# A hybrid DeltaNet, gating and Fourier step: chunk preparation a chunk ahead, a woven block inverse, and products one step behind

## The chip, the core and the metric

The kernel runs on one core of a Trainium2 chip. A core has a matrix engine (TensorE, PE in the profile; PEld is its weight load), three engines for elementwise work (VectorE or DVE, ScalarE or ACT, GpSimd or POOL) and SyncE (SP), which here only starts DMA transfers. Each engine runs its own list of instructions in order, and they wait for each other by semaphores. POOL and ACT can start transfers too. The metric is the device time of one execution in microseconds (us), lower is better.

## The reference, cut to what matters

One layer is computed for 2048 sample tokens and 128 prompt tokens, 1024 channels wide. A modulated RMSNorm gives `xn`; one input projection feeds three branches, each with its own SiLU gate; the branches are projected to 1024 channels, merged with sigmoid gates, and one output projection follows.

```python
proj = jnp.einsum('btd,de->bte', xn, w_in)
qkv, beta, dec, z_a, u_b, v_b, z_b, x_c, z_c, gates = jnp.split(proj, points, axis=-1)
# A: gated DeltaNet, forward and backward, with a triangular solve per chunk
m = eye + bc[..., :, None] * jnp.einsum('bnhik,bnhjk->bnhij', kc, kc) * dec_strict
sol = lax.linalg.triangular_solve(m, rhs, left_side=True, lower=True, unit_diagonal=True)
...
o_a = rmsnorm(o, o_norm_g) * silu(z_a)
# B: spatial gating in chunks of 128 tokens, 4 groups of 128 channels
vs = jnp.einsum('gpq,bnqgc->bnpgc', w_s, rmsnorm(v)) + b_s
o_b = u * vs * silu(z_b)
# C: Fourier mixing over a 32 x 64 grid and the 128 channels of each of 4 groups
o_c = fftn(x_c, axes=(rows, cols, channels)).real * silu(z_c)
merged = sum_n sigmoid(gates_n) * (br_n @ w_branch_n);  out = merged @ w_out
```

The outputs are the normed tokens of both groups and the prompt's final DeltaNet states.

## The kernel before, in words

**Number format.** Large products run in float16 with a split of each operand into a high and a low half (three matmuls for one product). A weight panel is loaded as float32 (`wst`, two buffers), then converted by `load_w` (L180): ACT squares it into `wlo` with a sum (L187), `scales` (L166) sends that sum through a small matmul with `ones16` (`wscb`) and shifts exponents on DVE (L173 to L177), ACT writes the high half `whi` (L189) and DVE the low half `wlo` (L190). Five converted panels are kept.

**Order of the stages.** After the modulation come the norm and transposes of the tokens with the gate of branch A, to about 150 us; the q, k, v projection with its convolution, to 438; branch B's spatial part (`for t in range(NCH)`, L893, one chunk of 128 tokens per step), to 568; branch B's gates (L913, four groups of channels by five tiles of tokens, `gate_unit`, L860), to 798; branch C (L936, four groups), to 1160; then `merge` (L1016) for branches B, C and A, to 1560, 1903 and 2157; then the output projection.

**Branch A beside them.** The DeltaNet work is a generator, `delta` (L842), advanced by `pace.tick(us)` calls inside the other stages: one step for every 1.6 us of work that the caller names. It first runs `prep` (L562) for all 17 chunks in five groups, four of four chunks and the prompt chunk last, and after each group `base_inverse` (L620); then `scan_dir` (L760) over the chunks forward and backward, where `level` (L660) builds a chunk's full 128 x 128 inverse from the 32 x 32 ones by two levels of products.

`prep` loads q, k and v of the chunk (`qr`, `kq`, L569), transposes them on TensorE, normalises q and k (square on ACT, sum on DVE, a power on POOL, L576 to L583), stores `kv` (L585), transposes k into `T` (L590), loads the decays `dc` (L594), and makes for both directions the matrices `n32` (L602) and their float16 halves `n16`, the diagonal blocks `nd` for the inverse (L604, L610) and `qk` (L616). Loads and stores all go to SP's queue but for `kT`.

`base_inverse` gathers the diagonal blocks of a group with eight loads (L633), inverts them by 31 pairs of products on DVE (L641, L642), makes a transposed copy (L645) and float16 halves of both (L649, L650), and stores the halves (`ei`, eight transfers, L655) and the float32 values (`es`, eight, L657). `level` loads them back as `ec` (L666) and `e3` (L668).

**What sets the order.** The program is recorded in the order of the Python code; a planner with an estimate of each instruction's duration then fixes the order on each engine and queue, and adds the semaphores. `tc.high_priority()` moves an instruction ahead; evictions of the product banks stand in it. There are three product banks (`ps_mm`), three for branch A and two others (`ps_x`). A pool that closes gives its memory to the next one, which then waits for the last users.

Of the kernel before, what the change touches and what calls it, by code (L numbers as in the profile page):

```python
# [110 lines left out]
def hybrid_flow_kernel(ctx: ExitStack, tc: tile.TileContext, x_prompt, x_sample, state_delta, c, c_ctx, ln_g, w_ada,  # L111
# [68 lines left out]
    def load_w(src, nkt, cols=P, hi=None, lo=None, tag="w", bufs=5):  # L180
        w = _W()
        st = sb(wp, [P, nkt, cols], "wst" if cols == P else tag + "st", bufs=2 if cols == P else 1)
        SY.dma_start(st, src.rearrange("(k p) c -> p k c", p=P))
        w.hi = sb(wp, [P, nkt, cols], tag + "hi", F16, bufs=bufs) if hi is None else hi
        w.lo = sb(wp, [P, nkt, cols], tag + "lo", F16, bufs=bufs) if lo is None else lo
# [38 lines left out]
    wdone, wnext = [], [0]  # L224

    def fetch(upto):
        while len(wdone) < min(upto, len(wlist)):
            src, nkt, tag, bufs = wlist[len(wdone)]
            wdone.append(load_w(src, nkt, tag=tag, bufs=bufs))
# [11 lines left out]
    class Pace:  # L241
# [6 lines left out]
        def tick(self, us):  # L248
            self.acc += us
# [153 lines left out]
    def decays():  # L403
# [69 lines left out]
        def rows_of(t):  # L473
            if t % 5 == 0:
                row = sb(dq, [P, 2, WB], "dc")
            elif t % 5 in (1, 2):
                row = sb(dq, [P, 1024], ("E", "Et")[t % 5 - 1]).rearrange("p (d x) -> p d x", d=2)
# [34 lines left out]
    for ct in range(12):  # L512
        w = getw(1, 2)
        for half in range(1):
# [20 lines left out]
            G.dma_start(qkvD[ct], y)  # L535
    pace.drain()
# [10 lines left out]
    GROUPS = [list(range(0, 4)), list(range(4, 8)), list(range(8, 12)), list(range(12, 16)), [16]]  # L547
    ndD = [dram(f"nd{g}", [2, P, len(ts), H, 32]) for g, ts in enumerate(GROUPS)]
    eD = [dram(f"ei{g}", [2, P, len(ts), H, P], F16) for g, ts in enumerate(GROUPS)]
    e32D = [dram(f"es{g}", [2, P, len(ts), H, 32]) for g, ts in enumerate(GROUPS)]  # L550
# [11 lines left out]
    def prep(g, ci, t):  # L562
        tok = sb(dq, [P, 2, WB], "tok")
        qr = sb(dq, [P, H, P], "qr")
        ss = sb(dq, [P, 2, H], "ss2", bufs=2)
        for part in range(3):
            ps = bank(ps_d, [P, WB])
            kq = qr if part == 0 else sb(dq, [P, H, P], "kq", bufs=2)
            SY.dma_start(kq, qkvD[part * 4:part * 4 + 4, :, chunk_off(t):chunk_off(t) + P].rearrange("h p t -> p h t"))  # L569
            for h in range(H):  # L570
                PE.transpose(ps[:, hs(h)], kq[:, h, :], ident)
            if part == 2:
                A.copy(tok[:, 1, :], ps)
                continue
            sq = sb(dq, [P, WB], "sq")
            A.activation(sq, ps, AF.Square)  # L576
            V.tensor_reduce(ss[:, part, :], h3(sq), AX.X, ALU.add)
            G.tensor_scalar(ss[:, part, :], ss[:, part, :], EPS, None, ALU.add)
            G.tensor_tensor(ss[:, part, :], ss[:, part, :], mhalf.to_broadcast([P, H]), ALU.pow)
            if part == 0:  # L580
# [310 lines left out]
    for i in range(4):  # L891
        V.tensor_copy(vinv[:, i:i + 1], vw[i].inv)
# [289 lines left out]
```

## Time and profile before

| | us |
|---|---|
| Time, median of 3 runs (range) | 2362.06 (2357.59 to 2364.58) |
| Profiled execution | 2355.22 |
| its span, first to last instruction | 2353.4 |
| TensorE busy | 2253.2 (96%) |
| VectorE busy | 1275.4 (54%) |
| ScalarE busy | 759.8 (32%) |
| GpSimd busy | 842.9 (36%) |
| Mean granted clock of TensorE | 0.985 |
| Moved by DMA | 350.39 MB, 149 GB/s on average |

"Span" runs from the first to the last instruction of the profiled execution. Groups of instructions are named by line, engine and operation, and `out<-in` are the program's names of tiles. "SPq" is SP's queue of transfers: the time in such a row is that of issuing the transfer, not that of moving its bytes. A wait is put down to the instruction that came last. The granted clock is the share of full speed that TensorE was given in that time: 1.00 or 0.50 here.

### The profile page before, as it was taken

How to read it: one execution, taken by the hardware profiler on the slowest of the kernel's cores; microseconds unless marked ns; L12 is line 12 of the kernel's file. 1: busy time of each engine (PE TensorE's matmuls, PEld its weight loads, DVE VectorE, ACT ScalarE, POOL GpSimd, SP SyncE). 2: the span in 40 equal slices, each digit the busy share in tenths (PEclk: the TensorE clock that was granted, in tenths of full speed). 3: DMA queues.
4: the chain of work that ended last, by engine and by line, in shares of the span. 5: the costliest groups of instructions: out<-in, count | busy, mean ns of one | idle time of the engine just before them, and what ended most of it. 6: DMA issues, size and time to landing. Idle time of an engine off the chain costs nothing. (4 is left out here: it accounts for less than half of the span.)

```text
span 2353.4 us, 43324 instructions
## 1 busy us (share of the span) xinstructions
PE 2253.2 (96%) x17092; PEld 1374.5 (58%) x17092; DVE 1275.4 (54%) x3015; ACT 759.8 (32%) x1426; POOL 842.9 (36%) x1056
## 2 busy tenths in 40 slices
PE   7999999999989987899989999999999999999998
PEld 3554444897545767779656656656665444444443
DVE  5638743568474867465665556665654242232444
ACT  3545533323323332232322222242322142221332
POOL 2422621344334430454422334455543112122543
PEclk9999999999999999999999999999999999999999
DMA  8316622575867662344444444565553353332542
GB/s 277 134 51 218 229 78 80 162 214 148 242 165 225 175 162 55 92 139 139 145 156 134 137 148 144 171 217 164 176 162 102 103 169 115 106 108 76 190 148 98
DMA packets 353237, 350.39 MB, mean 149 GB/s; under 512 B 70929, under 2 KB 273674, under 8 KB 351498
## 3 DMA queue, kind: packets, MB, share of 16 engines
q1 hardware_dynamic: 338986, 294.13, 41.6%
q0 software_dynamic: 9152, 40.13, 4.4%
q10 hardware_dynamic: 4896, 13.37, 1.6%
q8 instruction: 134, 2.20, 0.4%
q14 instruction: 69, 0.57, 0.1%
HBM read 222.16 MB, written 125.39 MB: 148 GB/s over the span
## 5 line engine op out<-in xcount | busy, mean ns | idle before, releaser
L160 PE MATMUL b<-xh,whi 128*128 128x512 f16 (+1 forms) x2080 | 704.1, 348 | 7.9 <-DVE sg L869 5.2
L160 PE MATMUL b<-xl,whi 128*128 128x512 f16 (+1 forms) x2080 | 705.2, 348 | 0.5 <-POOL xl L379 0.4
L160 PE MATMUL b<-xh,wlo 128*128 128x512 f16 (+1 forms) x2080 | 704.4, 348 | 0.2 <-DVE wlo L190 0.2
L160 PEld LDWEIGHTS <-whi 128*128 128x128 f16 x4160 | 389.0, 98 | 385.9 <-issue 17.4
L160 PEld LDWEIGHTS <-wlo 128*128 128x128 f16 x2080 | 204.1, 98 | 192.8 <-issue 5.3
L160 PE MATMUL b<-big,bhi 128*128 128x512 f16 (+1 forms) x960 | 252.6, 348 | 4.4 <-ACT big L1012 4.1
L1044 POOL TENSOR_TENSOR mrow<-mrow,sg 128x512 f32<-128x512 f32 (+1 forms) x80 | 88.0, 1104 | 316.0 <-DVE sg L1043 230.7
L160 PE MATMUL b<-whi,xh 128*128 128x128 f16 x1088 | 191.7, 222 | 1.5 <-DVE sg L869 1.5
L160 PE MATMUL b<-whi,xl 128*128 128x128 f16 x1088 | 191.8, 222 | 0.0
L160 PE MATMUL b<-wlo,xh 128*128 128x128 f16 x1088 | 191.8, 222 | 0.0
L160 PEld LDWEIGHTS <-xh 128*128 128x128 f16 x2312 | 179.6, 99 | 8.4 <-issue 7.4
L1034 ACT ACTIVATE sg<-b,winv 128x512 f32<-128x512 f32 (+1 forms) x120 | 74.6, 622 | 310.1 <-PE b L160 306.6
L160 PE MATMUL b<-big,blo 128*128 128x512 f16 (+1 forms) x480 | 163.5, 348 | 0.0
L1043 DVE SCALAR_TENSOR_TENSOR sg<-b,binv,sg 128x512 f32<-128x512 f32 (+1 forms) x80 | 53.4, 669 | 184.5 <-PE b L160 182.2
L777 POOL TENSOR_SCALAR skn<-skn,ed 128x128 f32<-128x128 f32 x136 | 81.1, 611 | 175.8 <-DMA skn<-kv 171.3
L534 POOL TENSOR_TENSOR cy<-cy,raw 128x545 f32<-128x545 f32 (+1 forms) x48 | 74.9, 1585 | 180.3 <-ACT raw L533 180.3
L160 PEld LDWEIGHTS <-bhi 128*128 128x128 f16 x960 | 89.3, 98 | 84.0 <-ACT big L1012 2.3
L160 PEld LDWEIGHTS <-xl 128*128 128x128 f16 x1224 | 115.2, 99 | 0.4
L677 POOL TENSOR_TENSOR R<-ec,cst 128x512 f16<-128x512 f16 x68 | 72.6, 1088 | 104.3 <-PE b L160 65.5
L160 PE MATMUL b<-wohi,mh 128*128 128x512 f16 x272 | 104.1, 383 | 2.1 <-ACT mh L1089 2.1
L160 PE MATMUL b<-wohi,ml 128*128 128x512 f16 x272 | 104.0, 383 | 1.6 <-DVE ml L1090 1.6
L160 PE MATMUL b<-wolo,mh 128*128 128x512 f16 x272 | 104.1, 383 | 0.0
(377 smaller groups left out, 3718.4 us busy)
## 6 DMA issues: line engine op xcount, KB each, us to landing
wst<-in_w_in_dram SPq DMA_DIRECT2D x60, 512.0 KB
qkv<-cy POOLq DMA_DIRECT2D x12, 1089.0 KB, 4.4
mrow<-br SPq DMA_DIRECT2D x24, 512.0 KB
mrow<-mrg SPq DMA_DIRECT2D x19, 512.0 KB
mrow<-mrg SPq DMA_DIRECT2D x16, 576.0 KB
mrg<-mrow POOLq DMA_DIRECT2D x16, 576.0 KB, 3.2
dc<-dec SPq DMA_DIRECT2D x17, 512.0 KB
kq<-qkv SPq DMA_DIRECT2D x34, 256.0 KB
```

Source lines behind the costliest of these rows:

```text
L160: PE.matmul(out, l, r, start=start, stop=stop)
L534: G.tensor_tensor(y[:, c0:c1], y[:, c0:c1], raw[:, 1 + c0:1 + c1], ALU.mult)
L677: G.tensor_tensor(dst[:, l].rearrange("p h a b c -> p h (a b) c"), wide(ec[:, :, which ^ d, l, :]), bm, ALU.mult)
L777: G.tensor_scalar(kn_[:, hs(h)], kn_[:, hs(h)], ed[:, d, t, h:h + 1], None, ALU.mult)
L1034: A.activation(sg, ps, AF.Sigmoid, scale=gw.inv)
L1043: V.scalar_tensor_tensor(sg, ps, binv[:, 1:2], sg, ALU.mult, ALU.mult)
L1044: G.tensor_tensor(mr, mr, sg, ALU.add)
```

## The change

Matmuls and their operands are the same, apart from how the 32 x 32 inverses reach `level`.

- **Chunk preparation.** While a chunk is prepared, the loads of the next one are issued (`held`; `rows`, `decay_rows`; `kq` three buffers, `qr` and `dc` two). k is now turned first, then v, then q. `kv` and `nd` are stored from POOL; the stores of `n16` and `qk` are held back by one (`late`). The prompt chunk comes first, as group 0.
- **Block inverse.** `base_inverse` of a group is woven between the steps of the next group's chunks. It keeps float32: the two copies are interleaved in `XB` and stored by eight transfers in four steps; `es` goes. `level` loads one float32 tile and makes the halves itself.
- **Weights.** `read_w` issues a panel's load, `convert` does the rest; `Pace.tick` issues reads up to two panels ahead, at the third tick after a conversion. The projection panels of the branches (`b`) are converted only once their own pool is open, with the first merge.
- **Branch B.** `w_spatial` is loaded at the end of the q, k, v stage. The product with `wsT` stands one chunk behind the projection, its store two more. The gate stage loads a whole row of 2176 tokens per group (`vrow`), a group ahead, instead of five pieces.
- **Branch C.** Its constants are loaded ahead of branch B. The first product of a step stands behind the next step's projection; the second and third are staggered in the same way.

```diff
+    def convert(st, nkt, cols=P, hi=None, lo=None, tag="w", bufs=5):
+        w = _W()
+        wpool = bwp[0] if tag == "b" else wp
...
+    def read_next():
+        if len(wread) < min(len(wdone) + 2, len(wlist)):
+            src, nkt, tag, bufs = wlist[len(wread)]
+            wread.append(read_w(src, nkt))
     def fetch(upto):
         while len(wdone) < min(upto, len(wlist)):
             src, nkt, tag, bufs = wlist[len(wdone)]
-            wdone.append(load_w(src, nkt, tag=tag, bufs=bufs))
+            if tag == "b" and not bwp:
+                return
+            if len(wread) == len(wdone):
+                read_next()
+            wdone.append(convert(wread[len(wdone)], nkt, tag=tag, bufs=bufs))
+            wlate[0] = 3
...
         def tick(self, us):
+            wlate[0] -= 1
+            if wlate[0] <= 0:
+                read_next()
...
+    wsn = sb(ep, [P, WB], "st", bufs=3).rearrange("p (g q) -> p g q", g=4)
+    SY.dma_start(wsn, w_spatial[0].rearrange("g p q -> p g q"))
...
-    GROUPS = [list(range(0, 4)), list(range(4, 8)), list(range(8, 12)), list(range(12, 16)), [16]]
+    GROUPS = [[16], list(range(0, 4)), list(range(4, 8)), list(range(8, 12)), list(range(12, 16))]
...
+    def late(dst, src):
+        if owed:
+            SY.dma_start(*owed.pop())
+        if dst is not None:
+            owed.append((dst, src))
+    def prep(g, ci, t, nxt, held):
...
+        more(1, lambda: rows(1, nxt))
+        more(0, lambda: rows(0, nxt))
+        ps = turned(1)
+        norm(ps, 1)
...
+        A.copy(tok[:, 1, :], turned(2))
+        more("dc", lambda: decay_rows(nxt))
+        norm(turned(0), 0)
...
-        SY.dma_start(kvD[t], tok)
+        G.dma_start(kvD[t], tok)
...
-            SY.dma_start(nD[d][t], n16)
+            late(nD[d][t], n16)
             yield 1
-        SY.dma_start(ndD[g][:, :, ci].rearrange("d p h i -> p d h i"), nd)
+        G.dma_start(ndD[g][:, :, ci].rearrange("d p h i -> p d h i"), nd)
...
     def base_inverse(g):
...
+        for _ in range(5):
+            yield 0
...
-        e16 = sb(dq, [P, 32, 2, 2, 32], "XB", F16)
-        for w_, src in enumerate((E, tmp)):
-            A.activation(e16[:, :, w_, 0, :], b3(src), AF.Copy, scale=FS)
-            V.scalar_tensor_tensor(e16[:, :, w_, 1, :], b3(src), FS, e16[:, :, w_, 0, :], ALU.mult, ALU.subtract)
+        both = XB.rearrange("p (j w c) -> p j w c", j=32, w=2)
+        V.tensor_copy(both[:, :, 1, :], E.rearrange("p (i j) -> p j i", j=32))
+        A.copy(both[:, :, 0, :], b3(E))
         yield 1
         for d in range(2):
             for B in range(4):
                 p0_ = d * 64 + B * 16
                 SY.dma_start(eD[g][d, 32 * B:32 * B + 32].rearrange("j t h c -> (t h) j c"),
-                             e16[p0_:p0_ + nb].rearrange("p j w l c -> p j (w l c)"))
-                SY.dma_start(e32D[g][d, 32 * B:32 * B + 32].rearrange("j t h c -> (t h) j c"), blk(E if d == 0 else tmp, d, B))
-        yield 1
+                             both[p0_:p0_ + nb].rearrange("p j w c -> p j (w c)"))
+                if B % 2:
+                    yield 1
     def level(d, t):
...
+        e32 = sb(dq, [P, H, 2, 32], "e32")
+        SY.dma_start(e32.rearrange("p h w c -> p h (w c)"), eD[g][d, :, ci])
         ec = sb(dq, [P, H, 2, 2, 32], "ec", F16)
+        A.activation(ec[:, :, :, 0, :], e32, AF.Copy, scale=FS)
+        V.scalar_tensor_tensor(ec[:, :, :, 1, :], e32, FS, ec[:, :, :, 0, :], ALU.mult, ALU.subtract)
...
     def delta():
+        for i_, (g, ci, t) in enumerate(seq):
+            if ci == 0 and g:
+                for r_ in base:
+                    if r_:
+                        yield 1
+                base = base_inverse(g - 1)
+            for n_, _ in enumerate(prep(g, ci, t, seq[i_ + 1][2] if i_ < 16 else None, held)):
+                yield 1
+                if n_ % 7 not in (2, 5) and next(base, 0):
+                    yield 1
...
     for t in range(NCH):                                  # branch B, spatial part
...
+        if vprev is not None:
+            spatial(*vprev)
+        if len(vout) > 2:
+            vstore()
         V.tensor_scalar(vn, vn, ss, None, ALU.mult)
-        ps = bank(ps_x, [P, 4, P])
-        for g in range(4):
-            mm(ps[:, g, :], vn[:, g, :], wsT[:, g, :])
...
+        vprev = (t, vn)
...
     for g in range(4):                                    # branch B, gates
         uw, zw = getw(2, 2)
+        vrow = vnext
+        if g < 3:
+            vnext = sb(vp, [P, NTOK], "vrow")
+            SY.dma_start(vnext, vsD[g + 1])
         for ti, (t0, tn) in enumerate(TBS):
-            st = sb(ep, [P, tn], "st", bufs=3)
-            SY.dma_start(st, vsD[g][:, t0:t0 + tn])
+            st = vrow[:, t0:t0 + tn]
...
     for g in range(4):                                    # branch C
...
+                if prev is not None:
+                    columns_of(*prev)
+                prev = (q, xc)
...
+            held = rows_in(0)
+            yp = columns_of(*prev)
+            for q4 in range(4):
+                nx = rows_in(q4 + 1) if q4 < 3 else None
+                rows_out(q4, held)
+                held = nx
...
     ms_ = ExitStack()
+    bwp.append(pool(ms_, "bwp", 1))
```

## The prediction

> **What bounds the kernel now.** I read the share of busy time first, then a table by stretch of the run, then the waits of TensorE in the stretches that the change edits, then the timeline around one long wait.
>
> ```profile
> PE 2253.2 (96%) x17092; PEld 1374.5 (58%) x17092; DVE 1275.4 (54%) x3015; ACT 759.8 (32%) x1426; POOL 842.9 (36%) x1056
> ```
>
> TensorE is the bound, but 96% does not say how much is left, because matmuls overlap. The spacing of their starts does. In the timeline below, two 512-column matmuls at full clock start 0.216 us apart (690.30 and 690.51) though each lasts 0.38. Elsewhere in that view 128-column fp16 matmuls start 0.056 apart, float32 ones 0.112, 64-column ones 0.030. By the counts of the profile (6960, 4800, 2762 and 2040; the rest, mostly 120 float32 ones of 256 columns, 40 us) that is 1503 + 269 + 309 + 61 + 40, about 2183 us of pure issue. From first to last matmul pass 2338 us, so some 153 us are lost. Spread by starts and spacings: 15 us before 150 (loading), 2 in 150 to 438 (q, k, v), 9 in 438 to 568 (branch B, spatial part), 26 in 568 to 798 (B, gates), 52 in 798 to 1160 (branch C), 12 in 1160 to 1210 (start of the first merge), 37 after it. The middle three make 87.
>
> The table by stretch (busy us of PE, PEld, DVE, ACT, POOL, then clock, DMA share, GB/s) shows the same places:
>
> ```profile
> 438.00:568.00 130.00, 123.31 (x1795) 118.57 (x1793) 91.29 (x242) 36.75 (x76) 52.81 (x106) 1.00 0.62 186
> 568.00:798.00 230.00, 211.91 (x1248) 120.42 (x1248) 148.30 (x360) 75.54 (x139) 92.98 (x151) 0.98 0.70 203
> 798.00:1160.00 362.00, 332.57 (x3681) 277.25 (x3679) 223.12 (x579) 112.38 (x263) 138.63 (x185) 0.96 0.44 122
> 1560.00:1903.00 343.00, 339.55 (x2408) 196.97 (x2407) 165.28 (x417) 100.61 (x205) 142.78 (x159) 1.00 0.48 152
> ```
>
> The waits of TensorE from 438 to 1160 (what it waited for, us, times, longest):
>
> ```profile
> PE b L160 <- DVE yp L959: 8.2, 2, 7.7
> PE b L160 <- DMA sqk<-qk: 8.1, 1, 8.1
> PE b L160 <- DVE sg L869: 6.7, 2, 5.2
> PE b L571 <- DMA qr<-qkv: 5.8, 3, 5.2
> PE b L160 <- ACT xc L949: 4.4, 3, 2.3
> PE b L160 <- DVE wscb L170: 3.4, 2, 2.0
> PE b L160 <- DVE sg L904: 3.2, 2, 3.1
> ```
>
> With the shorter ones they come to 53.6 us. After the longer waits the granted clock is 0.5 for 3.4, 6.8 or 10.2 us at a time; TensorE is busy 27.8 us at half rate there, which loses 13.9. So 67.5 of the 87 us are waits and their clock; the other 19.5 are small gaps between unlike matmuls, as the later stretches have too, and stay.
>
> The cause of the longest is one queue. The timeline around the 5.2 us wait (start, duration, engine, line, operation; in brackets the idle time before it and what ended it):
>
> ```profile
> 676.82 2.30 SPq L657 DMA_DIRECT2D es<-E  x4
> 679.53 4.08 SPq L657 DMA_DIRECT2D es<-Et  x4
> ...
> 683.72 7.26 SPq L655 DMA_DIRECT2D ei<-XB  x8
> ...
> 690.30 0.38 PE L160 MATMUL b<-xh,whi 128*128 128x512 f16 x1
> ...
> 690.51 0.38 PE L160 MATMUL b<-xl,whi 128*128 128x512 f16 x1
> ...
> 691.02 0.97 SPq L594 DMA_DIRECT2D dc<-dec  x1
> ...
> 691.92 1.06 PE L160 MATMUL b<-qr,T 128*128 128x128 f32 x8
> ...
> 696.88 0.61 DVE L602 SCALAR_TENSOR_TENSOR n<-b,beta,dc 128x128 f32<-128x128 f32 x2 [7.12 <-DMA dc<-dec]
> ...
> 698.20 0.59 PE L160 MATMUL b<-xh,whi 128*128 128x512 f16 x1 [5.22 <-DVE sg L869]
> ...
> 698.58 0.63 PE L160 MATMUL b<-xl,whi 128*128 128x512 f16 x1
> ```
>
> SyncE needs 14 us merely to issue the sixteen stores of one base inverse. The load of dc stands behind them, VectorE waits 7.12 us for dc with the eviction sg (L869) queued behind it, and TensorE runs out of banks. The same sixteen stores stand right ahead of the 7.7 us wait (911 us: the next group's nd loads are late, VectorE holds yp) and of the 8.1 us wait (968 us: the scan's first loads).
>
> **The change part by part.** The built order has the same 15,889 matmuls, so the floor stays at about 2183 and only waits can move.
>
> *Stores of the base inverse and chunk loads.* The eight es stores per group go (40 in all), with the 34 loads of e; sixteen loads of st become four; kv and nd, 34 issues, move to POOL: SyncE issues 884 transfers instead of 1008. The eight ei stores remain (7.26 us, the same bytes) but in four pairs with other issues between. All loads of a chunk are issued a chunk ahead: counted in matmul time along the built order, the q load led its transposes by 2.7 to 6 us in half of the chunks and every q, k or v load now leads by at least 9.2. I take as gone: 5.2 (sg), 7.7 (yp), 5.8 (qr), 6.3 (banks held by n, L602, and "issue", at 606 and 672 to 676) and 2.0 (w_spatial, now loaded early). The scan's start keeps its own wait: from the first ei store to the first scan matmul lay 10 us of matmul work (870.4 to 880.6 in issue time), now 11.6, and es no longer stands ahead (6.4 us). I take 4.8 of the 8.1 as gone. Sum 31.8, with the clock behind these waits 8.8. Bounds: 0, if the loads are late for another reason, and 31.8 + 3.3 + 10.5 = 45.6, if nothing is left.
>
> *Weight loads apart from conversion.* ACT's wait for wst no longer stands in the order right after its issue. Waits for wscb are 3.4, with 3.4 of clock (571 and 797). At the start of B's gates the order still converts a weight right ahead of its use (five buffers, all held), so I take half, 3.6; bounds 0 and 6.8.
>
> *One step behind.* B's product waited 3.2 for the scaled sg (L904), C's first product 4.4 for xc: 7.6 gone. In C the copies of Y1 and yp now have only 0.22 to 0.67 us of matmul work in front of their users, against 0.69 and 0.42 us for the copies: about 0.7 each, six times, 4 added. Bounds +9 and -2.
>
> *Float32 inverse.* Per group two ACT (1.06) and two DVE (1.27) conversions go; per scan step one of each of a quarter of the size comes, at 0.30 and 0.53 (rows of Q, L694 and L695): 10 us of ACT and 18 of DVE over 34 steps in a stretch where DVE is 60% busy. Zero; if that cover is gone, 18.
>
> *kv and nd on POOL.* 34 issues at 0.6 (24.3 us for 40 br stores), 20 us on an engine 40% busy; the next normalisation's power stands behind them. Between 0 and 20; I take 2, near the br row, whose issues delay nothing seen here.
>
> *Where the change adds a wait.* The b weights are converted only when the merge opens: the first use followed conversion by 98 us of matmul work and now by 3.6. The conversion is 0.15 x 4 on DVE and 0.6 to 1.2 on ACT, behind the o16 conversions. Between 0 and 8; I take 3. The early w_spatial load stands among the first weights: 256 KB at 277 GB/s, 1 us.
>
> Sum: 31.8 + 8.8 + 3.6 + 7.6 - 4 - 2 - 3 - 1 = 41.8. The profiled execution (2355.2; span 2353.4) would be 2313; the runs' median lies 6.8 above it, so the forecast is 2362 - 42 = **2320**. All upper ends together give 60, all lower ones -49.
>
> A page speaks to the clock term. The Trainium skill ("TensorE: Matmul & The Clock Gate", Why this matters for your kernels) asks for no idle gap over about 3 us between bursts, so a shorter wait should cost no clock. The trace differs: the clock was 0.5 from 797.1 to 800.5 after a wait of 2.0. By the rule my remaining waits would be free of clock and the sum nearer 47.
>
> **Rivals.** *Nearly all goes* (2295, gain 67, all waits and their clock): what speaks for it is that all the long waits have one queue behind them; against it, the order keeps tight spots.
>
> *The wait moves within the queue* (2347, gain 15): nd loads, ei stores and a whole-row vs load (1.1 MB where 256 KB were loaded) still take SyncE's time, 4 to 7 us in a row; the two longest waits then halve (8 with their clock 4) and the small ones go (3).
>
> *VectorE becomes late* (slower, 2377). Today preparation and inverse take turns; now the inverse's 31 pairs of products (L641 and L642, 0.35 and 0.38 each) are woven between a chunk's n, tok and the evictions, and the scan starts 37 us of matmul time earlier, so DVE's 64% in 568 to 798 becomes about 70%. TensorE's waits on DVE from 438 to 1160 are some 30 us; it decides once waits of that kind grow by the 42 gained, 1.4 times their size; at 57 more the kernel is 15 slower. Against it: in the two longest of the 30, DVE was itself waiting for a transfer.
>
> *POOL's transfers wait for VectorE* (2362, no change): if each of the 34 took 2.5 us more to issue, as long as a long VectorE copy (2.14, L645), and half of this came through to the normalisation, 42 us would be lost. In the trace POOL's issues beside a busy VectorE average 0.6. The Trainium skill ("SBUF — State Buffer", A bandwidth-pool intuition that's wrong, and the warning ahead of it) says that transfers issued from GpSimd starve while VectorE runs float32 copies, 620 ns growing to 3100; its remedy is the queue that the change leaves. No row here shows it.
>
> **How the numbers follow.** Forecast (2305 to 2337) 0.50, nearly all 0.14, moved within the queue 0.18, POOL no change 0.06, VectorE late 0.12. A measurement of this kernel tells 0.3% (7 us) from no change. Faster: 0.82; same 0.06; slower 0.12. The range from 2290 to 2358 takes in the first three and leaves out some two in ten.
>
> **What would show it.** Right: the sum of TensorE's waits between 438 and 1160 falls from 54 to about 20; no wait on sqk, qr or yp over 4 us; es gone from SyncE; fewer stretches at clock 0.5. Weights: no wscb wait except at the start of B's gates. Merge: a wait on bhi or blo of some 3 us at the start of the first merge. Wrong: long waits for L689 to L697, n32 or sg on VectorE, POOL issues over 1 us, or a clock of 0.5 as often as now.

## The result, and the profile after

The changed kernel takes **2336.09 us** (median of 4 runs, 2333.37 to 2342.83) against 2360.42 us (4 runs, 2357.59 to 2364.58) for the kernel before: ratio **0.990**, 95% interval 0.9873 to 0.9926. It is faster by 24 us. The forecast was 42 us faster, 2320, with a range of 2290 to 2358. The profiled execution took 2335.90 us (span 2334.1), 19.3 us less than the one before.

The share of busy time hardly moved; VectorE does 10 us less, GpSimd 18 us more:

```profile
PE 2250.1 (96%) x17092; PEld 1373.0 (59%) x17092; DVE 1265.1 (54%) x3039; ACT 766.5 (33%) x1455; POOL 861.1 (37%) x1090
```

The table by stretch of the changed kernel (same columns as before: busy us of PE, PEld, DVE, ACT, POOL, then clock, DMA share, GB/s), with one stretch more, in the first merge:

```profile
438.00:568.00 130.00, 124.67 (x1803) 120.40 (x1801) 96.97 (x266) 36.54 (x76) 61.94 (x116) 0.99 0.65 194
568.00:798.00 230.00, 220.18 (x1432) 130.29 (x1432) 161.49 (x415) 80.14 (x149) 108.03 (x186) 0.98 0.71 208
798.00:1160.00 362.00, 349.89 (x3870) 288.15 (x3870) 216.73 (x581) 121.48 (x297) 161.40 (x205) 0.98 0.44 130
1330.00:1525.00 195.00, 181.31 (x1413) 112.36 (x1411) 122.22 (x333) 55.79 (x131) 76.22 (x85) 0.96 0.48 145
```

The same stretch of the first merge in the kernel before:

```profile
1330.00:1525.00 195.00, 194.73 (x1545) 119.89 (x1543) 114.38 (x327) 51.59 (x117) 73.77 (x88) 1.00 0.49 150
```

Between 568 and 1160 TensorE is now busy 25.6 us more in the same 592 us: that is the gain. In the first merge it is busy 13.4 us less, at a clock of 0.96 where it was 1.00: there part of the gain is given back. Stretches in time do not line up between two kernels, so from here on I use the loss of the prediction (the spacing between the starts of successive matmuls beyond what their kind needs, half clock included), cut at the same amounts of issued matmul work in each kernel. The columns are us of that work:

| kernel | 0-404 load, q, k, v | 404-580 B spatial, start of gates | 580-740 B gates | 740-940 C, start of the scan | 940-1100 C, merge opens | 1100-1375 merge 1 | 1375-2190 rest | sum |
|---|---|---|---|---|---|---|---|---|
| before | 17 | 17 | 15 | 48 | 20 | **10** | 26 | 153 |
| after | 18 | 17 | **5** | **23** | 19 | **26** | 30 | 137 |

So 35 us were gained from B's gates to the start of the scan, and 16 us lost in the first merge. The sums differ by 16 us and the two profiled executions by 19.3; the other 3.2 lie behind the last matmul, which starts 11.5 us ahead of the end in the kernel before and 8.3 in the changed one. The waits of TensorE between 438 and 1160 come to 27.0 us, from 53.6, and the stretches at half clock there to 27.2 us, from 40.8. The first waits of that list in the changed kernel (what for, us, times, longest):

```profile
PE b L160 <- DVE X L1073: 5.4, 1, 5.4
PE b L608 <- DVE n L650: 4.0, 3, 2.2
PE b L160 <- DVE vs L970: 3.9, 1, 3.9
PE b L637 <- DVE tok L626: 2.3, 2, 2.1
PE b L160 <- DVE sg L1047: 1.8, 2, 1.3
```

The waits on `qr` and `sqk` are gone, and the 7.7 us on `yp` have become 1.8 on its copy (L1047, whose tile is called `sg` here). New is the wait for X (L1073). In the first merge (1150 to 1600) the list of the changed kernel opens with something that cost 0.2 us before, the sums of `gate_row`, which makes one block of the gate row in each of the first merge's eight blocks:

```profile
PE b L160 <- DVE st L325: 13.6, 4, 3.8
PE b L160 <- DVE u L851: 3.1, 1, 3.1
```

The last of these four waits, in the timeline of the changed kernel (start, duration, engine, line, operation):

```profile
1500.69 0.38 SPq L1172 DMA_DIRECT2D wst<-in_w_ada_dram  x1
...
1505.22 2.07 POOL L731 TENSOR_TENSOR T<-ec,cst 128x512 f16<-128x512 f16 x2
1505.99 1.38 DVE L323 TENSOR_SCALAR st<-wst,scT 128x128 f32<-128x128 f32 x2 [1.92 <-DMA wst<-in_w_ada_dram]
...
1511.77 0.60 DVE L325 SCALAR_TENSOR_TENSOR st<-wst,scT,st 128x128 f32<-128x128 f32 x2
...
1512.92 0.16 DVE L170 CAST wscb<-wss 128x1 bf16<-128x1 f32 x1 [0.55 <-ACT wlo L194]
1513.23 0.42 DVE L722 SCALAR_TENSOR_TENSOR ec<-e,ec 128x256 f16<-128x256 f32 x1 [0.15 <-ACT ec L721]
1513.27 2.35 POOL L731 TENSOR_TENSOR R<-ec,cst 128x512 f16<-128x512 f16 x2 [5.99 <-ACT ec L721]
1513.57 2.99 DVE L325 SCALAR_TENSOR_TENSOR st<-wst,scT,st 128x128 f32<-128x128 f32 x5
1516.35 0.64 PE L160 MATMUL b<-st,sel 128*2 128x128 f32 x4 [3.62 <-DVE st L325]
```

The panel is loaded at 1500.7, as soon as VectorE frees a `wst` buffer; its sixteen sums run from 1506.0 to 1516.6; TensorE stands 3.6 us at the matmul that reads them, 15.7 us after the load's issue. Two things make the sums slow: they stand behind other operations (here the next weight's `wscb` and the new `ec` product), and while POOL works on the scan's products (L731) single sums take 1.1 us instead of 0.34.

### The profile page after: what moved, and what is told of

Read it like the earlier page. It is cut to its first block, busy times and chain, and to the rows that moved or that the text cites. A ratio compares the mean times of both kernels' runs of the same rounds, so it can differ in the third digit from the quotient of the medians.

```text
span 2334.1 us, 43185 instructions
## 1 busy us (share of the span) xinstructions
PE 2250.1 (96%) x17092; PEld 1373.0 (59%) x17092; DVE 1265.1 (54%) x3039; ACT 766.5 (33%) x1455; POOL 861.1 (37%) x1090
## 5 line engine op out<-in xcount | busy, mean ns | idle before, releaser
L554 POOL TENSOR_TENSOR cy<-cy,raw 128x545 f32<-128x545 f32 (+1 forms) x48 | 69.0, 1464 | 192.9 <-ACT raw L553 192.9
L731 POOL TENSOR_TENSOR R<-ec,cst 128x512 f16<-128x512 f16 x68 | 75.6, 1129 | 85.4 <-PE b L160 61.4
```

Source lines behind the costliest of these rows:

```text
L554: G.tensor_tensor(y[:, c0:c1], y[:, c0:c1], raw[:, 1 + c0:1 + c1], ALU.mult)
L731: G.tensor_tensor(dst[:, l].rearrange("p h a b c -> p h (a b) c"), wide(ec[:, :, which ^ d, l, :]), bm, ALU.mult)
```

## The experiments

My theory after the result: the two `wst` buffers hold panels read ahead, so `gate_row` gets its panel late. The rival: VectorE does the sums late whatever the panel does. Beside that, parts of the change are undone or done alone, to price their terms. An edit of the text prices a part only if the planner's order moves with it, so where it did not, the run's paragraph says so. The changed kernel's own 2336 is the yardstick. All runs were timed against the kernel before, which came to 2360.0 to 2363.8 us beside them.

### gate_row's panel in tiles of its own

```diff
-        st = sb(wp, [P, KT, P], "wst", bufs=2)
-        SY.dma_start(st, w_ada_[...])
+        st = [sb(ep, [P, 512], "st", bufs=3).rearrange("p (k c) -> p k c", k=4) for _ in range(2)]
+        for i in range(2):
+            SY.dma_start(st[i], src[:, 4 * i:4 * i + 4, :])
```

> The changed kernel, with the w_ada panel of gate_row read into two buffers of its own (two of the three `st` tiles, which the first merge otherwise leaves idle) instead of a `wst` buffer. Theory (the panel is late because both `wst` buffers hold weight panels read ahead): TensorE's waits for gate_row's sums in the first merge, 13.6 us in four places in the changed kernel, fall below 2 us, the half clock behind three of them (13.6 us, 6.8 lost) goes with them, and the time falls from 2336 to about 2317 (2313 to 2322). Rival (VectorE does the sixteen sums too late, between evictions that have priority): the panel lands earlier, the waits stay over 8 us and the time is 2330 to 2340.

Measured: **2317.94 us** (2309.73 to 2322.13), ratio 0.9822 (0.9799 to 0.9846). The loss in the first merge falls from 26 to 9 us. TensorE's waits there (1150 to 1600), the longest and the one for the sums:

```profile
PE b L160 <- DVE mrow L1158: 2.5, 1, 2.5
...
PE b L160 <- DVE st L326: 0.5, 1, 0.5
```

With tiles of its own the panel is loaded some 90 us (blocks four to eight) before the matmul that uses its sums, and nothing waits for its sums. An earlier load takes the waits away, as the theory said. (The loss is that of the profiled execution, 2309.73 us, the fastest of the five.) What holds the `wst` buffers is left to the next run.

### No weight read ahead of its conversion

```diff
-            wlate[0] -= 1
-            if wlate[0] <= 0:
-                read_next()
```

> The changed kernel, with nothing read ahead of its conversion: a weight panel is read where it is converted, as in the kernel before (the b weights are still converted from the opening of the merge on). Theory (read-ahead panels hold both `wst` buffers against gate_row): the waits for gate_row's sums go, 13.6 us and 6.8 of clock, and the weights term of the prediction comes back, 3.6 us (0 to 6.8): 2336 - 20.4 + 3.6 = 2319 (2315 to 2324). Rival (reading ahead is worth more than was forecast, in B's gates, C and the merges): waits on wscb and whi come back for 10 us or more and the time is 2326 or above. Rival (the sums are late for VectorE's sake): the gate_row waits stay and the time is 2336 to 2343.

Measured: 2332.87 us (2328.32 to 2336.49), ratio 0.9888 (0.9867 to 0.9909). The waits for the sums stayed: 11.8 us in four, the loss in the first merge 25. But the edit did not take the reading ahead away. Between 438 and 1160 us a panel's load was issued a median of 21.6 us ahead of its conversion, 21.7 in the changed kernel and 19.6 in the kernel before, whose text reads nothing ahead: in the built order a load goes early wherever it stands in the text. So this run prices neither reading ahead nor its part in the late panel. The kernel before speaks against my theory: there, too, `gate_row`'s panel was loaded only 10 to 15 us ahead of the matmul (blocks three to eight); the sums then took 7 to 9 us from first to last and just made it. In the changed kernel's last four blocks they take 10.5 to 11.6. Why the `wst` buffer comes free no earlier stays open.

### kv and nd back on SyncE

```diff
-        G.dma_start(kvD[t], tok)
+        SY.dma_start(kvD[t], tok)
-        G.dma_start(ndD[g][:, :, ci]...)
+        SY.dma_start(ndD[g][:, :, ci]...)
```

> The changed kernel, with the kv and nd stores (34 issues) back on SyncE. Theory (every load of a chunk is issued a chunk ahead, so nobody waits for the some 17 us of issue time that come back, and POOL's issues, 0.5 us each, held nobody): 2336 plus or minus 5, with the loss between 568 and 1048 us within 5 of the changed kernel's. Rival (transfers from POOL wait for VectorE): faster by 10 or more. Rival (SyncE's queue is still tight): slower by 6 to 15, with waits on loads of chunk data.

Measured: 2318.85 us (2316.55 to 2321.78), ratio 0.9829 (0.9808 to 0.985). That is 17 us faster, as the rival on POOL's queue had it, but not by its mechanism: from 404 to 940 the loss is 47 us against 45 in the changed kernel. The gain is in the first merge (12 against 26) and just ahead of it (13 against 19): the waits for `gate_row`'s sums are gone, although nothing in the merge was edited. In the changed kernel POOL's issues of these stores were not slow (engine, operation, count, busy us and mean ns, idle time before):

```profile
L658 POOL DMA_DIRECT2D nd<-nd x17 | 13.4, 788 | 2.4 <-POOL nd L652 1.8 <-issue 0.2
L633 POOL DMA_DIRECT2D kv<-tok x17 | 10.7, 627 | 18.1 <-ACT tok L628 6.5 <-DVE tok L626 5.5 <-DVE sg L939 3.9
```

### Loads where they are used

```diff
-        more(1, lambda: rows(1, nxt))
-        more(0, lambda: rows(0, nxt))
+        cur[1] = rows(1, t)
...
-        dc, qr = cur["dc"], cur[0]
+        dc, qr = decay_rows(t), cur[0]
```

(The same for v and q.)

> The changed kernel, with the loads of q, k, v and dc of a chunk issued where they are used, as in the kernel before; float32 inverse, POOL stores, read-ahead weights and products one step behind stay. Theory (the loads that stand behind the stores of the base inverse make the waits; a chunk of lead hides them): waits on qr, dc (through n and the evictions behind it) and kq come back for 10 to 20 us with their clock, and the time is 2346 to 2360. Rival (halving the stores was enough, the lead is worth little): 2333 to 2341.

Measured: 2334.27 us (2330.1 to 2340.18), ratio 0.9895 (0.9873 to 0.9916); loss 3 in B's gates and 24 in C to the scan, as in the changed kernel (5 and 23). The time is the rival's, but the lead was not undone. A load of q and the transposes that use it, in the kernel before, the changed kernel and this run:

```profile
744.78 0.37 SPq L569 DMA_DIRECT2D qr<-qkv  x1
750.41 0.60 PE L571 MATMUL b<-cst,qr 128*128 128x128 f32 x4
```

```profile
690.26 0.37 SPq L587 DMA_DIRECT2D qr<-qkv  x1
721.47 0.60 PE L608 MATMUL b<-cst,qr 128*128 128x128 f32 x4
```

```profile
691.83 0.37 SPq L587 DMA_DIRECT2D qr<-qkv  x1
722.67 0.62 PE L608 MATMUL b<-cst,qr 128*128 128x128 f32 x4
```

Over the 17 chunks the q load is issued a median of 5.6 us ahead of its use in the kernel before, 35.7 in the changed kernel and 35.2 here; dc 12.1, 44.0 and 43.5. So this run is nearly the changed kernel once more, and says nothing of what the lead is worth. It seems that the larger sets of buffers, and not the place in the text, let the loads go early; the run with fewer buffers, below, bears that out.

### The float32 inverse alone, in the kernel before

```diff
-        e16 = sb(dq, [P, 32, 2, 2, 32], "XB", F16)
+        both = sb(dq, [P, 2048], "XB").rearrange("p (j w c) -> p j w c", j=32, w=2)
...
-                SY.dma_start(e32D[g][d, 32 * B:32 * B + 32]..., blk(E if d == 0 else tmp, d, B))
...
+        A.activation(ec[:, :, :, 0, :], e32, AF.Copy, scale=FS)
+        V.scalar_tensor_tensor(ec[:, :, :, 1, :], e32, FS, ec[:, :, :, 0, :], ALU.mult, ALU.subtract)
```

> The kernel before, with one part of the change alone: the inverse is stored as float32 in one set of stores (the es stores and their loads go, 40 and 34 transfers) and its fp16 halves are made in level. Theory (the es and ei stores of SyncE are what delayed VectorE's and TensorE's transfers, and the lead of a chunk, whose removal cost nothing, is not): the waits on sg, yp and sqk in the kernel before (5.2, 7.7, 8.1 us) shrink by half or go, and the time falls from 2360 to 2335 to 2348. Rival (the weaving of the inverse into the next group did it): 2355 to 2365. Beside that, if the new ec product on VectorE is what makes gate_row's sums late, TensorE's waits for those sums in the first merge, 0.2 us in the kernel before, come to 5 us or more here.

Measured: 2350.55 us (2345.4 to 2354.84), ratio 0.9957 (0.9941 to 0.9973): 10 us faster. The loss in B's gates falls from 15 to 9, in C only from 48 to 46, and the first merge rises from 10 to 17, with 4.0 us of waits for `gate_row`'s sums. Half as many stores on SyncE are worth something, but less than the theory had it, and the first sign of the merge's wait comes with this part.

### The inverse not woven

```diff
-                base = base_inverse(g - 1)
-            for n_, _ in enumerate(prep(...)):
-                yield 1
-                if n_ % 7 not in (2, 5) and next(base, 0):
-                    yield 1
+            for _ in prep(...):
+                yield 1
+            if ci == len(GROUPS[g]) - 1:
+                for r_ in base_inverse(g):
```

> The changed kernel, with the base inverse of a group run right after that group's chunks, as in the kernel before, and no longer woven into the next group; all else as changed. Theory (fewer stores did it, not the weaving): the loss of TensorE's spacing from branch B's gates to the scan stays within 6 us of the changed kernel's, and the time is 2330 to 2342. Rival (the weaving keeps the group's nd loads, inverse and stores from standing between VectorE's evictions): waits on sg, n and yp come back, 10 to 25 us slower, 2346 to 2361.

Measured: 2323.66 us (2319.99 to 2324.49), ratio 0.9841 (0.9826 to 0.9856). Neither case had this. From C to the start of the scan the loss rises from 23 to 36 us, with waits of this kind (740 to 960):

```profile
PE b L160 <- DVE wscb L170: 7.8, 2, 6.3
PE b L160 <- POOL T L731: 4.4, 1, 4.4
```

So the weaving is worth some 13 us there. Branch B is better without it (12 against 17 in its spatial part, 2 against 5 in its gates), so that from 404 to 940 us of work the weaving is worth some 5 us in all. But in the first merge the loss falls from 26 to 12: the `gate_row` waits went again, and the kernel came out faster than with the weaving.

### Products in step

```diff
-            if vprev is not None:
-                spatial(*vprev)
+            spatial(t, vn)
...
-                if prev is not None:
-                    columns_of(*prev)
-                prev = (q, xc)
+                yp = columns_of(q, xc)
...
-                nx = rows_in(q4 + 1) if q4 < 3 else None
-                rows_out(q4, held)
+                rows_out(q4, rows_in(q4))
```

> The changed kernel, with the products of B's spatial part and of C issued in step again instead of one step behind. Theory (the term of the prediction, 7.6 gained and 4 given): waits on sg's scaling (3.2) and xc (4.4) come back, waits on the copies of Y1, yp and X go, 2336 + 3.6 = 2340 (2334 to 2345). Rival (the step behind only moves the waits to the copies): 2328 to 2336.

Measured: 2324.07 us (2320.87 to 2327.8), ratio 0.9848 (0.9832 to 0.9864). In branch B's spatial part and in C the loss is the same as in the changed kernel (17 and 22 against 17 and 23): one step behind moves the waits and gains nothing. Here the order did move: the product with `wsT` starts a median of 0.4 us behind the scaling that it needs, 2.9 in the changed kernel, and C's first product a median of 1.0 us behind `xc`, 5.1 in the changed kernel. Of the 12 us, 9 come from the first merge (17 against 26), where one wait of 1.0 us for the sums is left, and some from the work just ahead of it.

### The low half of ec on POOL

```diff
-        V.scalar_tensor_tensor(ec[:, :, :, 1, :], e32, FS, ec[:, :, :, 0, :], ALU.mult, ALU.subtract)
         R = sb(dq, [P, WB], "R", bufs=2)
+        G.tensor_scalar(r4, e32, FS, None, ALU.mult)
+        G.tensor_tensor(ec[:, :, :, 1, :], r4, ec[:, :, :, 0, :], ALU.subtract)
```

> The changed kernel, with the low half of ec (the one new product that level has on VectorE, L722) made on POOL in two operations. Theory (L722 waits on VectorE for the load of e or for ACT's half, and what stands behind it there is late): TensorE's wait for X at the start of the scan (5.4 us, 3.4 of clock behind it) goes, and the waits for gate_row's sums in the first merge, where L722 stands among the sums, fall from 13.6 us to below 6; the time is 2314 to 2326. Rival (the sums are late for other reasons, the other operations of the scan and the next weight's scaling): 9 us at most, 2326 to 2334. Rival (POOL, with 68 operations more, becomes late for R and T): 2336 or above, with waits on R16 and T16.

Measured: 2317.12 us (2311.11 to 2319.07), ratio 0.9814 (0.9796 to 0.9831). The waits for the sums fell to 1.0 us, but the wait for X stayed. How it arises in the changed kernel, by the timeline:

```profile
888.05 7.14 SPq L707 DMA_DIRECT2D ei<-XB  x8
...
898.40 0.43 SPq L718 DMA_DIRECT2D e<-ei  x1
...
900.98 0.42 ACT L721 ACTIVATE ec<-e 128x256 f16<-128x256 f32 x1 [6.88 <-DMA e<-ei]
...
901.30 0.36 ACT L1072 COPY X<-b 128x260 f32<-128x260 f32 x1
901.49 0.88 DVE L722 SCALAR_TENSOR_TENSOR ec<-e,ec 128x256 f16<-128x256 f32 x1 [6.94 <-DMA sn<-n]
...
902.29 0.41 DVE L1073 COPY X<-b 128x252 f32<-128x252 f32 x1
...
902.76 0.58 PE L160 MATMUL b<-cf,X 128*128 128x128 f32 x1 [5.43 <-DVE X L1073]
```

The last group's eight `ei` stores fill SyncE for 7.1 us; the load that reads them back is issued 3.2 us after the last; ACT and VectorE reach the two new conversions (L721, L722) 7 us early and stand there, with C's copies of X behind them. With the low half on POOL, ACT's half still stood there:

```profile
901.93 0.42 ACT L721 ACTIVATE ec<-e 128x256 f16<-128x256 f32 x1 [7.55 <-DMA e<-ei]
...
902.65 0.42 DVE L1075 COPY X<-b 128x252 f32<-128x252 f32 x1 [7.81 <-ACT X L1074]
```

### The phase of the scan in the merge

```diff
+    pace.acc -= 3 * QUOTA
     merge(1, True, 20, gate_row)
```

> The changed kernel, with nothing edited but the phase of the woven scan against the blocks of the first merge: at the merge's opening the pace is set back by three of the scan's portions (4.8 us of matmul work). In the changed kernel the scan's u (L851) comes 5 to 7 us after gate_row's matmul in blocks five to eight, in the kernel before and in the runs without a wait 12 to 14 us after it. Theory (gate_row has 12 to 13 us from its panel's issue in every version, and is late only where the scan's VectorE work falls among its sums): the waits for the sums fall from 13.6 us to below 3, with their clock, the loss between 1100 and 1375 falls from 25 to 9 to 17, and the time is 2316 to 2326. Rival (the change made the panel or the sums late whatever the phase): 10 us or more of these waits stay, 2331 to 2340.

Measured: 2333.97 us (2330.44 to 2336.21), ratio 0.9886 (0.9867 to 0.9906); the waits for the sums stayed, 12.1 us in four. But the edit did not move what it was to move: u still comes 4.7 to 6.5 us after `gate_row`'s matmul in blocks five to eight (4.9 to 7.3 in the changed kernel). The scan stands where it stood in the changed kernel, so this run says nothing for or against.

### Neither lead nor weaving

The edits of "Loads where they are used" and "The inverse not woven" together.

> The changed kernel, with both the lead of a chunk for its loads and the weaving of the inverse undone; float32 inverse, POOL stores, chunk order, earlier constants, read-ahead and step behind stay. Theory (either of the two covers the same late transfers, so that undoing one alone cost nothing between 580 and 848): the loss there, 23 us in the changed kernel, 21 with either undone, 47 in the kernel before, rises to 33 or more, and the time is 2335 to 2355 (the weaving alone undone gave 2324). Rival (the rest of the change, fewer transfers, the row loads of vs and the earlier constants, took those waits away): the loss stays below 27, and the time is 2318 to 2332.

Measured: 2323.08 us (2321.38 to 2325.08), ratio 0.9841 (0.9821 to 0.9862). The loss in B's gates is 3, in C to the scan 38, and in the part of these two that the expectation names (580 to 848) 23. But again only the weaving went: q is loaded a median of 32.6 us ahead of its use, against 32.2 in the run with the weaving alone undone, whose time (2323.66) this one repeats. Whether lead and weaving stand in for each other is left open.

### gate_row's own tiles, and all of ec on POOL

The edit of `gate_own`, and both halves of ec made on POOL from a scaled copy in R.

> The changed kernel, with gate_row's panel in `st` tiles (2318 alone) and both halves of ec made on POOL, the high one from a scaled copy in R. Theory (X at the start of the scan waits because the new ec products stand ahead of its copies on ACT and VectorE while the load of e is late; with one half left on ACT the 5.5 us wait stayed): this wait goes with its clock, 2318 - 5.5 - 3.4 = 2309 (2304 to 2315). Rival (POOL, three operations more a step, makes T and R late): waits on R16 and T16 of 5 us or more, 2316 or above. Rival (TensorE waits for the scan's first T instead, because the load of e is as late as before): the wait of 5 us moves some us on, 2313 to 2320.

Measured: 2315.87 us (2314.71 to 2318.89), ratio 0.9814 (0.9791 to 0.9837), no different from `gate_own` alone (0.9822). The third case holds: the wait for X is gone, and TensorE waits at the same place (880 to 920) for the scan's first T, which needs the same late load:

```profile
PE b L160 <- POOL T L734: 6.8, 1, 6.8
```

### As many buffers as before

```diff
-        x = sb(d2, [P, H, P], "kq" if part else "qr", bufs=3 if part else 2)
+        x = sb(d2, [P, H, P], "kq" if part else "qr", bufs=2 if part else 1)
```

(And two for `n32` and `n16` instead of three, in the kernel with neither lead nor weaving.)

> The run with neither lead nor weaving (2323), with the chunk preparation's buffers as many as in the kernel before: one for q (two in the change), two for k and v (three), two each for n32 and n16 (three). Theory (the second buffers are what let loads and stores go early, since the planner moves a load ahead as soon as its buffer is free, wherever the text has it): waits on qr, kq and n come back, the loss between 580 and 848, 23 us with neither, rises to 31 or more, and the time is 2331 to 2345. Rival (the new order of k, v and q, the row loads of vs and the early constants did it): the loss stays below 27 and the time is 2318 to 2329.

Measured: 2333.69 us (2330.41 to 2340.7), ratio 0.9869 (0.9846 to 0.9892), against 0.9841 with the buffers: some 7 us, but the two intervals overlap. This is the one run in which most of the lead of q, k and v went: q is loaded a median of 8.2 us ahead of its use instead of 32.6, k and v 17.7 instead of 30.6; dc keeps its two buffers and its lead (43.7). Waits on qr come back, 2.7 us in three. But the loss between 580 and 848 is 24, not 31: the time is the theory's, the place is not. From 404 to 940 the loss rises by 4 (14 against 11 in B's spatial part, 4 against 3, 38 against 38); 6 us of the difference lie behind 1375, where the profiles of like kernels differ by as much. So the lead of q, k and v is worth some 4 us here, and that of dc was not undone in any run.

All of them together, by the loss:

| kernel | 0-404 | 404-580 | 580-740 | 740-940 | 940-1100 | 1100-1375 | 1375-2190 | sum | us |
|---|---|---|---|---|---|---|---|---|---|
| before | 17 | 17 | 15 | 48 | 20 | 10 | 26 | 153 | 2360 |
| b_float32 | 18 | 20 | 9 | 46 | 15 | 17 | 26 | 150 | 2351 |
| after | 18 | 17 | 5 | 23 | 19 | 26 | 30 | 137 | 2336 |
| joined | 20 | 15 | 4 | 24 | 17 | 25 | 27 | 131 | 2333 |
| not_ahead | 19 | 19 | 3 | 24 | 19 | 28 | 24 | 136 | 2334 |
| phase | 19 | 19 | 5 | 25 | 19 | 26 | 23 | 135 | 2334 |
| on_sync | 19 | 17 | 9 | 22 | 13 | 12 | 26 | 117 | 2319 |
| not_behind | 19 | 17 | 3 | 22 | 17 | 17 | 31 | 125 | 2324 |
| not_woven | 18 | 12 | 2 | 36 | 15 | 12 | 30 | 125 | 2324 |
| neither | 19 | 11 | 3 | 38 | 17 | 13 | 27 | 126 | 2323 |
| few_buffers | 19 | 14 | 4 | 38 | 15 | 13 | 33 | 135 | 2334 |
| ec_pool | 18 | 15 | 4 | 29 | 17 | 12 | 25 | 120 | 2317 |
| best | 20 | 16 | 5 | 25 | 19 | 11 | 22 | 117 | 2316 |
| gate_own | 17 | 18 | 3 | 23 | 20 | 9 | 19 | 111 | 2318 |

The first merge splits them in two. In `after`, `joined`, `not_ahead` and `phase` the scan's u comes 5 to 8 us after `gate_row`'s matmul in blocks five to eight, and three or four of these blocks wait 2.2 to 3.9 us. (In the first four blocks, too, this distance is the same in the four to within 2 us: they are nearly one order, and count as one case more than as four.) In `on_sync`, `not_woven`, `not_behind`, `neither`, `few_buffers` and `ec_pool` it comes 12 to 18 us after it, and no such block waits over half a microsecond. `gate_own` has 5.6 to 7.3, the bad distance, and no wait: with the panel early the distance does not matter. So the times of `on_sync`, `not_woven`, `not_behind` and `neither` show how the merge fell out more than what the undone part is worth: that they are 12 to 17 us faster was not aimed at.

## Why the prediction was right or wrong, point by point

The side and the range were right. Profile against profile, 19.3 us came of the 41.8 forecast. The step that failed is "37 after it" (the loss behind the merge's start) taken as staying: the first merge lost 16 us more, as told under `gate_row` below. Ahead of the merge 33 us of some 46 priced were gained, and there the cause is only in part shown. The rest are small differences elsewhere. Two counts in it are off and change no sum: the profiles have 17,092 matmuls in both kernels, not 15,889, and twenty loads of `st` became four, not sixteen.

**Stores of the base inverse and chunk loads (31.8 and 8.8 of clock).** With the smaller terms the sum had some 46 us of gain from 404 to 1048 us of work; the traces show 33 (87 to 54). The loads are issued a chunk ahead, as it says (q 35.7 us ahead of its use instead of 5.6), and the waits that they were to remove are gone. That the lead removed them is not shown: two runs that were to undo it left it in place, and the one that took most of it from q, k and v lost some 4 us. From 404 to 940 the loss fell by 35 us (80 to 45). The parts tried give there 5 for the float32 inverse alone, 5 for the weaving, 4 for the buffers of q, k and v and 2 for kv and nd; each was measured in another kernel, so that even these 16 need not add up. The lead of dc, the order of k, v and q, the prompt chunk first, the row loads of `vs`, the early constants and the held-back stores were not undone, and what more than half of this gain comes from stays open. One detail failed: the `ei` stores were said to go "in four pairs with other issues between". In the trace they went as one block of eight in three of five groups (8.7, 9.6 and 7.1 us of SyncE) and nearly so in a fourth; only one group was spread.

**The scan's start (4.8 of 8.1).** The wait on `sqk` went and 5.4 us for X came, with its clock: 2.7 us of waiting gained instead of 4.8. The mechanism was not the one priced: not the scan's first loads, but conversions that wait for one of them, in ACT's and VectorE's order ahead of C's copies.

**Weights apart (3.6).** The wait for `wscb` fell from 3.4 to 0.8 us, 2.6 us of waiting. What did it is open: `joined`, which was to undo the reading ahead, left the loads where they were.

**One step behind (7.6 less 4).** Undone, the loss in B's spatial part and in C stays where it is: 0, inside its bounds of +9 and -2.

**Float32 inverse (0, or 18 without cover).** The cover held in the steady scan, but not at two places: at the scan's start, as said, and in the first merge, where the ec product stands among the sums of `gate_row`. The prediction priced its time and not its place.

**kv and nd on POOL (-2).** POOL issued them in 0.63 and 0.79 us (0.6 was taken), and with the stores back on SyncE the loss up to 940 us of work differs by 2. The rival "POOL's transfers wait for VectorE" needed 2.5 us more for each; no issue took over 0.82. That does not settle what the Trainium skill ("SBUF — State Buffer", A bandwidth-pool intuition that's wrong) says of transfers from GpSimd beside VectorE's float32 copies: only one of the 34 issues ran beside a float32 copy of VectorE's from SBUF to SBUF (L701; the issue took 0.64 us).

**b weights converted late (-3), w_spatial early (-1).** No wait on bhi or blo came, and the opening of the merge lost no more than before (940 to 1100: 19 against 20). 0 instead of -3. The early load of `w_spatial` was not undone.

**What was missing: `gate_row`.** 13.6 us of waiting and half the clock for 13.6 us behind it, 16 us of loss. The prediction said that "37 after it" (the loss behind the merge's start) stay, and costed nothing there, because the change edits nothing there. But its cover was thin in the kernel before: a panel loaded 10 to 15 us ahead of its matmul, with 4 to 5 us to land and 7 to 9 us of sums. What used it up, in the traces: in blocks five to eight of the changed kernel 15 of the 64 sums took 0.51 to 1.14 us instead of 0.34, 11.2 us more in all, and each of the 15 lay beside one of POOL's products of ec (L731, 1.05 to 1.5 us each). In the run with kv and nd on SyncE one sum of the last four blocks was slow, by 0.35. The two lines of the sums from 1330 to 1525, min, median and longest in ns, the changed kernel first:

```profile
L325 DVE SCALAR_TENSOR_TENSOR st<-wst,scT,st x56: 335/339/1142, 1346.4 to 1516.2; 128x128 f32<-128x128 f32 x56
```

```profile
L325 DVE SCALAR_TENSOR_TENSOR st<-wst,scT,st x56: 336/346/695, 1346.0 to 1495.6; 128x128 f32<-128x128 f32 x56
```

That the late panel is what exposes TensorE to this is shown by `gate_own`. That the distance between scan and block decides whether the sums meet POOL's products is argued, not shown: it fits these blocks of all runs but one (the float32 inverse alone had 6.7 us in three of them without a wait, and a wait of 2.0 at 13.4); in `ec_pool` eight sums of these blocks took 0.5 to 1.22 us at 17 to 18 us, without a wait; blocks three and four have 7.3 to 7.6 us in several runs without a wait, and the run that was to move the distance alone did not move it.

**The rivals.** Nearly all goes: no. The wait moves within the queue (2347): partly; the `ei` blocks and the late load at the scan's start are that case. VectorE late (2377): the mechanism appeared, in another stage and at a third of the price.

## What to carry to other kernels

When a change edits one stage and another stage is woven beside the same stream, look for the steps of the untouched stages whose cover is a few us, here a 512 KB panel loaded 13 us ahead of use from a shared rotation of two buffers, and give them a buffer of their own before pricing anything: this one edit was worth 18 us, where the whole change had brought 24. And undo a term before believing it: the step behind came to nothing, though the waits that it was aimed at had gone. But see in the trace that the order moved. Where a planner fixes the order, an edit of the text may move nothing: four of these runs left the loads or the scan where they were, and their unchanged times say nothing of the part. A conversion moved behind a load inherits the load's lateness, and so does what stands behind it on its engine; moving it to another engine only moved the wait.

## What the runs showed of the hardware

A sum of VectorE that starts while one of POOL's products of ec runs can wait for it rather than share with it: each of the fifteen slow sums of blocks five to eight ends 0.08 to 0.15 us after the end of the product that ran when it started (a sum from 1513.57 to 1514.71, the product from 1513.27 to 1514.56), and takes 0.51 to 1.14 us instead of 0.34. The Trainium skill ("SBUF — State Buffer", Who interferes with whom) says that a VectorE instruction with two SBUF inputs contends with a GpSimd instruction that reads SBUF, and that only an exclusive lock on a shared pair of ports makes engines wait for each other. Ten of the fifteen slow sums are of that form (L325) and agree. The other five (L323, `tensor_scalar`) read one tile and a column of factors; the same section has `tensor_scalar` contend only in a mode that uses both ports, and no row here shows the mode. Twelve other sums in the first merge that overlapped such a product ran at full speed, seven of them beside one product that itself took 2.35 us, so overlap alone does not decide.

The clock again fell after a short wait. In the changed kernel TensorE waited 2.1 us for `tok`, ending at 486.5, and the granted clock was 0.5 for 3.4 us after it; a wait of 2.5 us for `gate_row`'s sums that ended at 1409.1 was followed by a clock of 1.00, and so was one of 3.1 us for `sg` (L904) that ended at 529.1 in the kernel before. The table by stretch behind the three (PE, PEld, DVE, ACT, POOL, then clock), the changed kernel first:

```profile
486.40:490.00 3.60, 3.53 (x23) 3.50 (x24) 3.20 (x11) 1.31 (x3) 2.78 (x6) 0.53 0.96 318
1409.10:1413.00 3.90, 3.90 (x24) 2.34 (x25) 1.53 (x4) 1.30 (x3) 0.00 (x0) 1.00 0.61 166
```

```profile
529.10:533.00 3.90, 3.87 (x60) 3.86 (x61) 3.69 (x14) 0.00 (x0) 0.00 (x0) 1.00 0.01 2
```

So no single length of a wait decides it in these runs.
